# Gates and modulation vectors as sums along the row: one part of a two-layer diffusion block on one core

## The chip, the core and the metric

The kernel runs on one core of a Trainium2 chip. The core has five engines with an instruction queue each: TensorE (PE, matmuls, with its weight loads shown as PEld), VectorE (DVE), ScalarE (ACT), GpSimd (POOL) and SyncE (SP), and 16 DMA engines that move data between the chip's memory and the core's own. An engine runs its own queue in order; engines wait for each other through semaphores. The metric is the device time of one execution in microseconds. Before the change the median of three runs is 1769.55 us (1769.22 to 1769.56).

## What is computed

Two layers over 256 latent tokens with 2048 channels; the first also reads 256 context tokens. Each layer turns a conditioning vector into a shift, a scale and a gate per channel:

```python
def adaln(cond, w, b):
    m = jax.nn.silu(cond) @ w + b
    return jnp.split(m, 3, axis=-1)

def modulate(h, shift, scale):
    return h * (1 + scale) + shift

for i in range(DEPTH):                                   # DEPTH = 2
    shift, scale, gate = adaln(c, ada_w[i], ada_b[i])    # ada_w[i]: 2048 x 6144
    h = modulate(rms_norm(x, norm_g[i]), shift[:, None], scale[:, None])
    ...
    y = na_ssd_mixer(h, hc, ...) if i % 2 == 0 else short_conv_mixer(h, ...)
    x = x + gate[:, None] * y
```

The first layer's mixer has a wide input projection, 16 heads of neighbourhood attention, a bidirectional state-space scan, and an output projection. The second layer's has an input projection of 8192 columns, a short convolution, and an output projection. Everything is fp32.

The change concerns one thing: the products of the vector `silu(c)` with those parts of `ada_w` that aren't needed at the start. These are the first layer's gate (2048 columns) and the second layer's shift, scale and gate (6144 columns), 8192 columns in all, 64 MB of weights. The shift and scale of the first layer are made another way, at the start, and stay as they are.

## The kernel before

**Matmuls and weights.** Each fp32 weight is split into a high part in the format fp32r (ScalarE, L419) and the rest (VectorE, L426), and each product is made of three matmuls: high by high, low by high, high by low. L194 is the helper that records every matmul, L198 the one that records every transpose. Weights come in blocks of 128x1024 (512 KB) from SP's queue (L380 and L382) into buffers called `raw`: five of them, and four more at the start. A block waits there until one of three places `w` (six in the last part) is free, is split into it, used, and gives the place back.

**The order.** No scheduler runs on the chip. The program is laid out when it is built: generators for each piece of work say what they wait for, and a planner with its own cost for each instruction (class `Plan`, L38) decides which may put its next instructions on which engine. There are three lists, `urgent`, `side` and `back`. The vector-matrix products stand in `back`, the last to be asked (L283). When one generator changes, what the planner sees changes, and the instructions of all engines may be laid out anew.

**The products of the vector.** `later_loads` (L504) puts 128 loads of 128x1024 into a list: 16 groups `n` of 512 columns, eight loads `k` each, with two blocks of 128 rows beside each other, so that a partition holds two runs of 512 columns. `issue` (L364) sends them in among the ordinary weights, one or two under way at a time (`ngem`). `gemv_gen` (L799) consumes them, two groups at a time:

- VectorE clears `acc`, 128x1024 (L803). SP loads the bias, 512 numbers, into the first partition of each half (L808).
- For each load VectorE runs two instructions (L817) of 512 columns: weights times the channel's entry of `silu(c)` (the vector lies across the partitions in `csil`), plus `acc`.
- TensorE sums `acc` over the partitions with eight matmuls against ones (L825), VectorE copies the result to `rowb` (L827), and ScalarE's queue stores it as a row in `mrow` in the chip's memory (L830).
- After group 11 the shift and scale of the second layer are read back from there, transposed by TensorE into a column tile `M1` and copied (L835 to L840).

`n_back` says how far this has come. The gate of the first layer (from 3 on) is read in `res_gen` (L1587), `M1` (from 11.5 on) in `turn_gen` (L1625) and in `norm_gen` behind it, the gate of the second layer (from 15 on) in `fin_gen` (L1957). Gates are read from `mrow` as a row that is copied to all partitions.

**The rows that the prediction's steps touch.** L194, L198: matmuls and transposes. L419, L426: the split of a weight block. L603: the same kind of multiply-and-sum along the row that the change uses, in the norm of the input. L613, L628: the norm's scaling and the copy of its transposed tiles, at the start. L1910 to L1921: the second layer's gating. L1161: the first use of `rows` in the scan's time steps.

## Time and profile before

| | us |
|---|---|
| median of three runs | 1769.55 |
| profiled execution | 1768.15 |
| its span | 1766.2 |
| TensorE busy | 1742.5 |
| VectorE busy | 1260.7 |
| ScalarE busy | 773.2 |
| VectorE, the sums of L817 | 191.6 |
| VectorE, idle until a load of `ada_w` came | 64.2 |
| moved by DMA | 374.60 MB, mean 212 GB/s |

The profile is one execution. "Busy" is the time in which an engine has at least one instruction under way. Matmuls are pipelined and their ends are modelled, so the distance from one start to the next is the better measure of their cost. A group's line gives its line in the kernel, engine, operation, output and inputs with their shapes, the count, busy us and mean ns of one, and then the idle time of the engine just ahead of these instructions, with what ended it. The chain of waits follows the work that ended last backwards, at each step to what released it. A wait's line reads: who waited, for whom, us in all, times, longest. A line of the view by tile gives the shortest, median and longest duration in ns, and the first and the last start in us. Names lose their buffer numbers, so `tmp<-dram_csr` is any buffer `tmp` loaded from `dram_csr`.

### The profile page before, as it was taken

The page shows a single profiled execution, that of the slowest core. Times are in us where ns is not written, and L with a number is a line of the kernel's source. Part 1 is how long each engine was busy: PE and PEld are TensorE (multiplying, and loading weights), DVE is VectorE, ACT ScalarE, POOL GpSimd, SP SyncE. Part 2 cuts the span into 40 slices and gives each one's busy share as a digit, 9 for nine tenths or more (in the row PEclk, how much of TensorE's full clock was granted, in tenths as well). Part 3 has the DMA queues.
Part 4 walks back from the last instruction along what each step waited for, and adds up shares of the span by engine and source line. Part 5 has one row for each costly group of instructions (what it writes and reads, how often), then busy time and mean ns, then how long its engine had stood idle before and what let it go on. Part 6 is the DMA issues. An engine that isn't in the chain of part 4 may idle for free.

```text
span 1766.2 us, 25384 instructions
## 1 busy us (share of the span) xinstructions
PE 1742.5 (99%) x9577; PEld 1464.8 (83%) x9577; DVE 1260.7 (71%) x1986; ACT 773.2 (44%) x1330; POOL 32.1 (2%) x28
## 2 busy tenths in 40 slices
PE   6999999999999999999999999999999999999998
PEld 4777988888888889888888898888888888888887
DVE  5657778878686878675878787787668776555554
ACT  5423544455242445342445344565445444444442
POOL 0000100001000001000001000000000000000000
PEclk9999999999999999999999999999999999999999
DMA  9977644666746666646666566667867877666563
GB/s 369 347 283 253 209 148 134 200 207 203 233 141 199 205 199 194 220 134 195 209 189 190 159 189 198 194 207 273 294 212 239 264 260 250 189 187 189 190 210 120
DMA packets 218138, 374.60 MB, mean 212 GB/s; under 512 B 32304, under 2 KB 69008, under 8 KB 218016
## 3 DMA queue, kind: packets, MB, share of 16 engines
q1 hardware_dynamic: 210704, 366.38, 64.1%
q10 hardware_dynamic: 7312, 6.61, 1.1%
q8 instruction: 75, 1.23, 0.3%
q14 instruction: 47, 0.39, 0.1%
HBM read 367.52 MB, written 6.72 MB: 212 GB/s over the span
## 4 chain that ended last, share of the span: by engine, by line
PE 90%; DMA 5%; DVE 4%; issue 1%; SPq 1%; ACT 1%; POOL 0%; DVEq 0%; ACTq 0%
PE bank L194 86%; PE bank L198 3%; DMA raw<-in_ada_w 2%; DVE acc L817 1%; DVE w L426 1%; DMA tmp<-dram_csr 1%; DMA raw<-in_w_in 1%; DMA raw<-in_ada 0%; DVE tmp L1241 0%; DMA raw<-in_sc_in 0%; DMA half<-in_rows 0%; SPq L1045 0%; DMA acc<-in_ada_b 0%; ACT w L419 0%; DVE tmp L981 0%
## 5 line engine op out<-in xcount | busy, mean ns | idle before, releaser
L419 ACT CAST w<-raw 128x1024 fp32r<-128x1024 f32 (+1 forms) x343 | 358.2, 1046 | 536.4 <-PE bank L194 458.9
L426 DVE TENSOR_TENSOR w<-raw,w 128x1024 fp32r<-128x1024 f32 (+1 forms) x343 | 414.8, 1213 | 179.7 <-ACT w L419 178.4
L194 PE MATMUL bank<-hH,w 128*128 128x256 f32 (+1 forms) x2064 | 489.2, 324 | 2.5 <-DVE w L426 2.5
L194 PE MATMUL bank<-w,hH 128*128 128x512 f32 x1280 | 405.8, 395 | 2.6 <-ACT hH L757 2.6
L194 PEld LDWEIGHTS bank<-hH,w 128*128 128x128 f32 x2064 | 345.0, 188 | 36.0 <-DVE w L426 3.5
L194 PE MATMUL bank<-hL,w 128*128 128x256 f32 (+1 forms) x1040 | 334.3, 322 | 0.0
L194 PEld LDWEIGHTS bank<-w,hH 128*128 128x128 f32 x1280 | 236.6, 188 | 54.6 <-issue 4.6
L194 PE MATMUL bank<-w,hL 128*128 128x512 f32 x640 | 249.3, 390 | 0.1
L817 DVE SCALAR_TENSOR_TENSOR acc<-raw,csil,acc 128x512 f32<-128x512 f32 x256 | 191.6, 748 | 74.7 <-DMA raw<-in_ada_w 64.2
L194 PEld LDWEIGHTS bank<-hL,w 128*128 128x128 f32 x1040 | 196.4, 189 | 14.9
L194 PE MATMUL bank<-w,h 128*128 128x512 f32 x768 | 180.1, 391 | 0.0
L194 PEld LDWEIGHTS bank<-w,h 128*128 128x128 f32 x768 | 143.4, 188 | 29.8 <-issue 0.4
L194 PEld LDWEIGHTS bank<-w,hL 128*128 128x128 f32 x640 | 120.1, 188 | 25.4 <-DVE hL L763 0.6
L194 PE MATMUL bank<-w,mix 128*128 128x512 f32 x588 | 138.8, 392 | 0.0
L194 PEld LDWEIGHTS bank<-w,mix 128*128 128x128 f32 x588 | 109.4, 188 | 22.6 <-issue 0.2
L1241 DVE SCALAR_TENSOR_TENSOR tmp<-bank,cwh,tmp 128x508 f32<-128x508 f32 (+1 forms) x96 | 71.1, 744 | 1.8
L194 PE MATMUL bank<-KL,h 128*128 128x512 f32 x264 | 63.9, 389 | 0.0
L194 PEld LDWEIGHTS bank<-KL,h 128*128 128x128 f32 x264 | 49.5, 188 | 10.2
L426 DVE TENSOR_TENSOR wL<-raw,wH 128x1024 fp32r<-128x1024 f32 x31 | 37.9, 1222 | 27.6 <-ACT wH L419 27.5
L194 PE MATMUL bank<-QT,h 128*128 128x512 f32 x168 | 55.9, 391 | 0.0
L194 PE MATMUL bank<-wH,h 128*128 128x512 f32 x168 | 55.6, 390 | 0.0
L426 DVE TENSOR_TENSOR QL<-raw,QT 128x1024 fp32r<-128x1024 f32 x32 | 39.1, 1222 | 23.1 <-ACT QT L419 22.6
(288 smaller groups left out, 1976.8 us busy)
## 6 DMA issues: line engine op xcount, KB each, us to landing
raw<-in_w_in SPq DMA_DIRECT2D x196, 512.0 KB, 4.1
raw<-in_ada_w SPq DMA_DIRECT2D x128, 512.0 KB, 4.3
raw<-in_sc_in SPq DMA_DIRECT2D x128, 512.0 KB, 4.6
raw<-in_w_out SPq DMA_DIRECT2D x64, 512.0 KB, 4.2
raw<-in_ada SPq DMA_DIRECT2D x36, 512.0 KB, 5.4
raw<-in_sc_out SPq DMA_DIRECT2D x32, 512.0 KB, 3.7
PT<-in_ada SPq DMA_DIRECT2D x16, 512.0 KB, 8.6
tmp<-dram_csr SPq DMA_DIRECT2D x32, 256.0 KB, 5.8
```

Source lines behind the costliest of these rows:

```text
L194: E(T.matmul(o, l, r, start=start, stop=stop, skip_group_check=True))
L198: E(T.transpose(o, i, ident if k == 128 else ident[:k, :k]))
L419: E(S.copy(H, v))
L426: E(V.tensor_tensor(out=Lo, in0=v, in1=H.bitcast(F32), op=ALU.subtract))
L817: E(V.scalar_tensor_tensor(out=acc, in0=v[:, j], scalar=csil[:, 2 * k + j:2 * k + j + 1], in1=acc, op0=ALU.mult, op1=ALU.add))
L1241: E(V.scalar_tensor_tensor(out=do, in0=di, scalar=cwh[:, 32 * k + ch:32 * k + ch + 1], in1=do, op0=ALU.mult, op1=ALU.add))
```

## The change

The weights of these products are laid out anew on the host: block `m` of 128 output channels lies across the partitions, one channel to each, and the 2048 rows of the matrix lie along the row, in two halves of 1024. A load is still 128x1024, now in one piece. VectorE multiplies a block with `silu(c)`, which lies as a row in all partitions (`csb`), and sums along the row, in one instruction (L824 of the changed kernel). The result is one column of `gp` for each load. The two halves are added, then the bias, from a tile that is there anyway.

```diff
+    GEM = (range(0, 16), range(16, 48), range(48, 64))
...
-        for n in range(16):
-            lay = 0 if n < 4 else 1
-            c0 = 4096 + n * 512 if n < 4 else (n - 4) * 512
-            for k in range(8):
-                later.append(("g", ("gem", n, k), ada_w[lay], k * 256, 2, c0, 512))
+        for q, blocks in enumerate(GEM):
+            for h in range(2):
+                for m in blocks:
+                    later.append(("g", ("gem", m, h), adaT, 2 * m + h, 1, 0, 1024))
...
-    mrow = drt([4, D], "mrow")
+    mrow, crow = drt([2, D], "mrow"), drt([1, D], "crow")
     M1 = st([128, 2, KB], "M1")
-    accs = st([128, 2, 512], "acc")
+    csb = st([128, 1024], "csb")
+    gp = st([128, 2, 64], "gp")
+    rowt = st([128, 128], "rowt")
+    gcol = st([128, KB], "gcol")
...
+    def rows_out(col, dst):
+        yield W_("PE", col, nb=1)
+        ps = bank()
+        turn(ps[:16, :128], col)
+        yield W_("DVE", ps)
+        E(V.tensor_copy(rowt[:16, :], ps[:16, :128]))
+        give(free_b, ps)
+        yield W_("AQ", rowt)
+        E(DMA2.dma_start(dst.rearrange("(b c) -> b c", c=128), rowt[:16, :]))
...
     def gemv_gen():
-        for n2 in range(0, 16, 2):
-            yield W_("DVE", nb=0)
-            E(V.memset(accs, 0.0))
-            for n in (n2, n2 + 1):
...
-                    for j in range(2):
-                        if j:
-                            yield W_("DVE", acc)
-                        E(V.scalar_tensor_tensor(out=acc, in0=v[:, j], scalar=csil[:, 2 * k + j:2 * k + j + 1], in1=acc,
-                                                 op0=ALU.mult, op1=ALU.add))
+        yield from rows_out(csil[:, 0:KB], crow[0])
+        for q, blocks in enumerate(GEM):
+            for h in range(2):
+                yield W_("SP", crow, csb)
+                E(DMA.dma_start(csb, crow[0, h * 1024:(h + 1) * 1024].partition_broadcast(128)))
+                for m in blocks:
+                    yield when(lambda: ("gem", m, h) in RAW)
+                    yield W_("DVE", RAW["gem", m, h][0], csb)
+                    raw, _ = RAW.pop(("gem", m, h))
                     ngem[0] -= 1
+                    E(V.tensor_tensor_reduce(out=raw, in0=raw, in1=csb, scale=1.0, scalar=0.0, op0=ALU.mult, op1=ALU.add,
+                                             accum_out=gp[:, h, m:m + 1]))
                     give_raw(raw)
                     issue()
-            yield W_("PE", accs, nb=1)
-            ps = bank()
-            for m in range(2):
-                for g in range(4):
-                    mm(ps[32 * g:32 * g + 32, m * 128:(m + 1) * 128], ONES[:, :32], accs[:, m, g * 128:(g + 1) * 128], m == 0, True)
...
+            yield W_("DVE", gp)
+            p2 = lambda lo, n: (gp[:, 0, lo:lo + n], gp[:, 1, lo:lo + n])
+            if q == 1:
+                a, b = p2(16, 32)
+                o = M1.rearrange("p r b -> p (r b)")
+                E(V.tensor_tensor(out=o, in0=a, in1=b, op=ALU.add))
+                E(V.tensor_tensor(out=o, in0=o, in1=P_("ab1")[:, 0:32], op=ALU.add))
+            else:
+                a, b = p2(0 if q == 0 else 48, 16)
+                E(V.tensor_tensor(out=gcol, in0=a, in1=b, op=ALU.add))
+                E(V.tensor_tensor(out=gcol, in0=gcol, in1=P_("ab0" if q == 0 else "ab1")[:, 32:48], op=ALU.add))
+                yield from rows_out(gcol, mrow[q // 2])
+            n_back[0] = (3, 11.5, 15)[q]
```

The order of the parts stays: first layer's gate (`q` 0, 32 loads), second layer's shift and scale (`q` 1, 64 loads, straight into `M1`), second layer's gate (`q` 2, 32 loads). `csb` holds one half of the vector, so it is loaded six times, and each load has to wait for the last pass over the half before. The two gates, and `silu(c)` itself at the beginning, go through `rows_out`: a transpose on TensorE (16 columns of 128 to 16 rows), a copy on VectorE, a store from ScalarE's queue. The rest of the kernel is as before.

More of the change, by code (lines that the diff above doesn't have):

```diff
@@ L141, with kernel @@
 @with_exitstack
-def kernel(ctx: ExitStack, tc, x, cx, ada0, w0, ada_w, ada_b, w_in, w_out, sc_in, sc_out, rpb, small, const,
+def kernel(ctx: ExitStack, tc, x, cx, ada0, w0, adaT, w_in, w_out, sc_in, sc_out, rpb, small, const,
                        strict, rows, out):
@@ L378, in issue @@
             v = raw[:, :nb * n].rearrange("p (b c) -> p b c", b=nb)
-            if w is ada0 or w is w0:
+            if w is ada0 or w is w0 or w is adaT:
                 E(DMA.dma_start(raw, w[r0]))
@@ L791, in part_gen @@
         got.add(("part", j, key, t))
-    mrow = drt([4, D], "mrow")
+    mrow, crow = drt([2, D], "mrow"), drt([1, D], "crow")
     M1 = st([128, 2, KB], "M1")
-    accs = st([128, 2, 512], "acc")
+    csb = st([128, 1024], "csb")
+    gp = st([128, 2, 64], "gp")
+    rowt = st([128, 128], "rowt")
+    gcol = st([128, KB], "gcol")
     n_back = [0]
-    def gemv_gen():
-        for n2 in range(0, 16, 2):
-            yield W_("DVE", nb=0)
-            E(V.memset(accs, 0.0))
-            for n in (n2, n2 + 1):
-                lay = 0 if n < 4 else 1
-                c0 = 4096 + n * 512 if n < 4 else (n - 4) * 512
-                acc = accs[:, n - n2, :]
-                E(DMA.dma_start(acc[:1, :], ada_b[lay:lay + 1, c0:c0 + 512]))
-                for k in range(8):
-                    yield when(lambda: not (("gem", n, k) not in RAW))
-                    yield W_("DVE", RAW["gem", n, k][1], acc)
-                    raw, v = RAW.pop(("gem", n, k))
-                    ngem[0] -= 1
-                    for j in range(2):
-                        if j:
-                            yield W_("DVE", acc)
-                        E(V.scalar_tensor_tensor(out=acc, in0=v[:, j], scalar=csil[:, 2 * k + j:2 * k + j + 1], in1=acc,
-                                                 op0=ALU.mult, op1=ALU.add))
@@ L819, in gemv_gen @@
                     give_raw(raw)
                     issue()
-            yield W_("PE", accs, nb=1)
-            ps = bank()
-            for m in range(2):
-                for g in range(4):
-                    mm(ps[32 * g:32 * g + 32, m * 128:(m + 1) * 128], ONES[:, :32], accs[:, m, g * 128:(g + 1) * 128], m == 0, True)
-            yield W_("DVE", ps)
-            E(V.tensor_copy(rowb, ps[:, :256]))
-            give(free_b, ps)
-            yield W_("AQ", rowb)
-            E(DMA2.dma_start(mrow[n // 4, (n2 % 4) * 512:(n2 % 4) * 512 + 1024].rearrange("(m g c) -> g m c", m=2, g=4),
-                             two(rowb[0:128:32, :])))
@@ L832, in gemv_gen @@
-            n_back[0] = n
-            if n == 11:
-                yield W_("AQ", mrow[2:3, 1024:])
-                E(DMA2.dma_start(mrb[:32, :], mrow[1:3, :].rearrange("r (b c) -> (r b) c", c=128)))
-                yield W_("PE", mrb, nb=1)
-                pm = bank()
-                turn(pm[:, :32], mrb[:32, :])
-                yield W_("DVE", pm)
-                E(V.tensor_copy(M1.rearrange("p r b -> p (r b)"), pm[:, :32]))
-                give(free_b, pm)
-                n_back[0] = 11.5
@@ L844 @@
-    rowb = st([128, 256], "rowb")
-    mrb = rowb[:, :128]
+            yield W_("DVE", gp)
[10 more added lines that the diff above has]
+                yield from rows_out(gcol, mrow[q // 2])
@@ L1960, in fin_gen @@
         gb, o = tmp(), tmp()
-        yield W_("SP", mrow[3:4])
-        E(DMA.dma_start(gb, mrow[3, cols].partition_broadcast(128)))
+        yield W_("SP", mrow[1:2])
+        E(DMA.dma_start(gb, mrow[1, cols].partition_broadcast(128)))
         for t in range(2):
@@ L1995 @@
     force(lambda: not urgent, (urgent,))
-_INS = ['x', 'cx', 'ada0', 'w0', 'ada_w', 'ada_b', 'w_in', 'w_out', 'sc_in', 'sc_out', 'rpb', 'small', 'const', 'strict', 'rows']
+_INS = ['x', 'cx', 'ada0', 'w0', 'adaT', 'w_in', 'w_out', 'sc_in', 'sc_out', 'rpb', 'small', 'const', 'strict', 'rows']
 def kernel(**inputs):
@@ L2038 @@
                    for j in range(8) for c in (COL_K, COL_V, COL_Q)]).reshape(24, 128, 1024)
+    adaT = np.concatenate([f('ada_w')[0][:, 4096:], f('ada_w')[1]], axis=1).reshape(2, 1024, 64, 128).transpose(2, 0, 3, 1)
+    adaT = adaT.reshape(128, 128, 1024)
     arr = {
-        'x': f('x')[0], 'cx': f('ctx')[0], 'ada0': ada0, 'w0': w0, 'ada_w': f('ada_w'), 'ada_b': f('ada_b'), 'w_in': f('na_ssd_w_in')[0],
+        'x': f('x')[0], 'cx': f('ctx')[0], 'ada0': ada0, 'w0': w0, 'adaT': adaT, 'w_in': f('na_ssd_w_in')[0],
         'w_out': f('na_ssd_w_out')[0], 'sc_in': f('sc_w_in')[0], 'sc_out': f('sc_w_out')[0], 'rpb': f('na_rpb')[0],
```

## The prediction

> **What bounds the kernel now.** I read the page first: share of each engine, granted clock, the chain that ended last.

> ```profile
> span 1766.2 us, 25384 instructions
> PE 1742.5 (99%) x9577; PEld 1464.8 (83%) x9577; DVE 1260.7 (71%) x1986; ACT 773.2 (44%) x1330; POOL 32.1 (2%) x28
> PEclk9999999999999999999999999999999999999999
> PE 90%; DMA 5%; DVE 4%; issue 1%; SPq 1%; ACT 1%; POOL 0%; DVEq 0%; ACTq 0%
> ```

> TensorE is busy 99% of the span at full clock, and 90% of the chain is its own work. A microsecond of TensorE work is therefore a microsecond of the result, and work on VectorE costs time only where TensorE ends up waiting for it. Next I read the waits of TensorE that VectorE ended (first three rows; TensorE's other long wait, for the first weights, is at the start), and where they stand in the chain in order of time (start, length, what).

> ```profile
> PE bank L194 <- DVE w L426: 2.5, 2, 1.8
> PE bank L194 <- DVE tmp L1426: 1.1, 1, 1.1
> PE bank L198 <- DVE sgL L1916: 0.7, 1, 0.7
> ...
> 230.44 5.51 DMA half<-in_rows
> 236.40 1.21 DVE w L426
> 237.66 25.76 PE bank L194 x131
> ...
> 807.09 5.60 DMA raw<-in_ada_w
> ...
> 814.35 3.71 DMA raw<-in_ada_w
> ...
> 819.72 3.67 DMA raw<-in_ada_w
> ...
> 825.47 3.28 DMA acc<-in_ada_b
> ...
> 835.71 1.22 DVE w L426
> ...
> 842.56 7.82 PE bank L194 x64
> ...
> 1400.08 4.41 DMA raw<-in_ada_w
> ```

> All that VectorE holds TensorE up after the start is 2.5 + 1.1 + 0.7 = 4.3 us. The 1.8 us at 237 has nothing to do with the change: VectorE had sat behind the load of `rows`. The other 0.7 of the first row (842 us) and the 0.7 before 1410 us end stretches in which VectorE waited, again and again, for a load of `ada_w` that a sum over L817 needs, with the split of the weights (L426) queued behind it.

> **The change part by part.** The groups it touches (line, engine, operation, count | busy us, mean ns | idle before):

> ```profile
> L817 DVE SCALAR_TENSOR_TENSOR acc<-raw,csil,acc 128x512 f32<-128x512 f32 x256 | 191.6, 748 | 74.7 <-DMA raw<-in_ada_w 64.2 <-DMA acc<-in_ada_b 7.0
> L803 DVE MEMSET acc<- 128x1024 f32 x8 | 7.3, 912 | 1.3 <-issue 0.8 <-DVE half L1128 0.2 <-DMA raw<-in_w_in 0.2
> L827 DVE COPY rowb<-bank 128x256 f32<-128x256 f32 x8 | 3.4, 419 | 5.9 <-PE bank L194 5.9
> L194 PE MATMUL bank<-acc,const 128*32 128x128 f32 x128 | 5.2, 279 | 0.0
> L603 DVE CUSTOM_DVE_ANT_0 tmp<-x 128x512 f32<-128x512 f32 x8 | 5.3, 684 | 0.0
> L426 DVE TENSOR_TENSOR QL<-raw,QT 128x1024 fp32r<-128x1024 f32 x32 | 39.1, 1222 | 23.1 <-ACT QT L419 22.6
> ```

> *TensorE, removed.* 128 records are 8 groups of 16. Their mean of 279 ns is a modelled end; the price is read from start to start:

> ```profile
> 481.54 0.39 PE L194 MATMUL bank<-hL,w 128*128 128x512 f32 x1
> 481.77 0.39 PE L194 MATMUL bank<-hH,w 128*128 128x512 f32 x1
> 482.09 0.64 PE L194 MATMUL bank<-acc,const 128*32 128x128 f32 x16
> 482.66 0.50 PE L194 MATMUL bank<-hH,w 128*128 128x512 f32 x1
> 483.00 0.40 PE L194 MATMUL bank<-hL,w 128*128 128x512 f32 x1
> ...
> 1107.16 0.39 PE L194 MATMUL bank<-w,hL 128*128 128x512 f32 x1
> 1107.48 0.24 PE L198 MATMUL bank<-const,rowb 32*128 32x32 f32 x1
> 1107.65 0.73 PE L194 MATMUL bank<-w,hH 128*128 128x512 f32 x2
> 1108.22 0.39 PE L194 MATMUL bank<-w,hL 128*128 128x512 f32 x1
> ```

> Wide matmuls start 0.23 us apart. Without the group the one at 483.00 would start at 481.77 + 2 x 0.23 = 482.23, so a group costs 0.77 us, the change of shape on both sides included. Eight cost 6.2 us. The one transpose of `rowb`, by the same reading, costs 1108.22 - (1107.16 + 3 x 0.23) = 0.37 us. Removed: 6.6 us.

> *TensorE, added.* Three transposes of a 128x16 column tile (`csil`, and `gcol` twice). They are not in the trace; the nearest row is that 0.37 us. Bounds: 0.1 us each (a transpose that starts in step with its neighbours) to twice the row, 0.74. I take the row: 1.1 us in all, with 0.3 to 2.2 as ends. Net on TensorE: **-5.5 us** (-6.3 to -4.4).

> *VectorE.* Removed: 191.6 + 7.3 + 3.4 = 202.3 us. Added: 128 multiply-and-sum passes over 128x1024. The same operation over 128x512 takes 684 ns (L603), an elementwise pass over 128x1024 1222 ns (L426); I take 1.22 us. Each has a second instruction that reads the sum out:

> ```profile
> L603 DVE DVE_READ_ACCUMULATOR2_ANT ssq<- x8: 81/82/83, 6.7 to 35.9; 128x1 f32 x8
> ```

> So 1.30 us for each load of weights against 2 x 0.75 before: 166 us, and about 2 us for the few small additions and copies. Net -34 us, and nothing of it is on the path by itself. What it is worth are parts of the 4.3 us. The waits for `ada_b` (7.0 us of VectorE, among them the 3.28 us at 825) go; the memsets go; a cycle in the stretch before 842 gets 0.2 us shorter. In the changed program the last sum also stands behind 301 splits of weights instead of 357, so the stretch before 1410 us holds none. I count those two stalls as gone, -1.4 us. But the instructions of all engines are laid out anew by the planner, and a new layout has stalls of its own: VectorE-ended ones came to 4.3 us before. I add 0.7 us. Net **-0.7 us**; ends -4.3 (no such stall left) and +4.3 (twice as many).

> [...]

> *Loads and queues.* The 128 loads stay 512 KB each on SP, now with 4 KB in a row per partition. Gone are 16 small `ada_b` loads from SP and 8 row stores and a load from ScalarE's queue; new are 3 row stores there, and 6 broadcasts of 512 KB into `csb` on SP.

> ```profile
> raw<-in_ada_w SPq DMA_DIRECT2D x128, 512.0 KB, 4.3
> tmp<-dram_csr SPq DMA_DIRECT2D x32, 256.0 KB, 5.8
> ```

> A broadcast has to wait for the last pass over the old `csb`; SP holds every later weight load behind that, and the next pass on VectorE waits for the landing, with the splits queued behind it. The nearest price is between the two rows, 4.3 to 5.8 us. The first comes before any pass; five are exposed. In the stretch before 842 us the four waits shown above (5.60 to 3.28 us) held VectorE so within 22 us, and TensorE lost 0.7 us at its end, because it had split weights in hand. I cost five single waits at 0; ends 0 and five times that 0.7, +3.5 us. Without the cover each would cost its landing.

> *Start.* The store of `crow` is new in ScalarE's order, ahead of L628.

> ```profile
> 31.79 0.72 ACT L613 ACTIVATE x<-x,rx 128x512 f32<-128x512 f32 x1
> ...
> 32.41 0.38 PE L198 MATMUL bank<-const,x 128*128 128x128 f32 x2
> 32.82 0.27 ACT L628 COPY xm<-bank 128x128 f32<-128x128 f32 x1 [0.31 <-PE bank L198]
> ```
> ```profile
> L830 ACTq DMA_DIRECT2D dram_mrow<-rowb x8: 532/532/1092, 382.1 to 1498.8; - x8
> ...
> L1962 SPq DMA_DIRECT2D tmp<-dram_mrow x4: 423/468/1740, 1696.5 to 1744.3; - x4
> ```

> L628 waits for TensorE anyway, and the 0.53 us of an issue (L830) can run in the sequencer while L613 computes: 0; at most what 0.31 us of idle time leaves of it, 0.2. The memset that goes, at the place of the new copy, was the longer one.

> *Later.* The last row was stored at 1499 us and is first read at 1697; in the changed program the sums end earlier still. The first gate is finished at the same place in the order as before. Both stay covered, cost 0; uncovered, the price would be the whole lateness.

> Sum: -5.5 - 0.7 = **-6.2 us**. The profiled execution took 1768.15 us, its span and 1.95 around it; that gives 1761.95. The median of the runs lies 1.40 us above the profiled execution, so the prediction for the median is **1763.3 us**.

> **The rivals.** What a measurement of this kernel can tell from no change is about 0.2%, 3.5 us: below 1766.0 is faster, above 1773.1 slower.

> *The saved TensorE time turns into waiting.* The new layout has about twice the VectorE stalls and some broadcasts show: -5.5 + 4.3 + 1.5 is about 0, 1769. For it: the order was laid out anew everywhere. Against it: VectorE has 34 us less to do. [...] Chance 0.20.

> *More is won.* All VectorE stalls but the one behind `rows` go and the transposes cost little: -6.3 - 2.5 - 1, about 1760 or below. Chance 0.10.

> *Slower: the swap of `csb`.* At each of the five swaps SP holds the weight loads until VectorE has caught up, and VectorE holds the splits until 512 KB have landed; TensorE runs out. It decides from (5.5 + 3.5) / 5 = 1.8 us a swap. At 3 us a swap, about half the landing, it is +15 - 5.5: 1779. For it: VectorE waited 64 us for such loads before. Against it: four within 22 us cost 0.7. Chance 0.13.

> [...] Chance 0.05.

> **How the numbers follow.** The forecast keeps 0.52. Its own bounds are 1759 to 1768. Faster: 0.50 of the forecast, 0.10, and 0.05 of the first rival, 0.65. Same: 0.17. Slower: 0.13 + 0.05 = 0.18. The range for 8 in 10 is 1758.5 to 1771: the forecast, most of the gain case and the first rival; it leaves the slower ones out.

> **What would show it.** Right: the 16-matmul groups are gone and nothing stands in their place, so TensorE's busy time falls by about 5.5 us with no more idle time; the multiply-and-sum rows show about 1.22 us and 0.08; VectorE's busy time falls by some 34 us; no wait of TensorE traces back to `csb`. Wrong: new waits of TensorE for L427 (the old L426) behind a pass that waited for `csb` or a load; rows of 2 us; a later first wide matmul than at 34 us.

## The result, and the profile after

| | before | after |
|---|---|---|
| median, us | 1769.38 (six runs, 1767.05 to 1770.01) | 1786.65 (six runs, 1783.88 to 1789.53) |
| ratio, with its 95% interval | | 1.0101 (1.0086 to 1.0116) |
| profiled execution, us | 1768.15 | 1783.88 |

The changed kernel is 17 us slower; 6 us faster was predicted. The page of the changed kernel, with the lines that were read first before (span, busy time by engine, granted clock, shares of the chain):

```profile
span 1782.1 us, 25025 instructions
PE 1761.9 (99%) x9451; PEld 1467.8 (82%) x9451; DVE 1224.5 (69%) x1978; ACT 773.0 (43%) x1330; POOL 31.6 (2%) x28
PEclk9999999999999999999999999999999999999999
PE 98%; DVE 1%; DMA 1%; ACT 0%; issue 0%; SPq 0%; POOL 0%; DVEq 0%; ACTq 0%
```

TensorE has 126 matmul records fewer, and is busy for 19.4 us longer, at full clock (1.0 granted in both). It isn't waiting either: its own work is now 98% of the chain, against 90%. So the loss lies inside the work that the change doesn't touch. The new work itself looks as forecast. Its groups (count | busy us, mean ns | idle before), and then, from the waits of TensorE (us in all, times, longest), the only one that VectorE ends:

```profile
L824 DVE CUSTOM_DVE_ANT_0 raw<-raw,csb 128x1024 f32<-128x1024 f32 x128 | 155.4, 1219 | 21.3 <-DMA raw<-in_adaT 19.1 <-DMA csb<-dram_crow 1.9
L824 DVE DVE_READ_ACCUMULATOR2_ANT gp<- 128x1 f32 x128 | 10.5, 82 | 0.0
```

```profile
PE bank L195 <- DVE w L427: 0.9, 1, 0.9
```

A pass takes 1219 ns and its read-out 82, the swaps of `csb` cost VectorE 1.9 us in all, and what VectorE holds TensorE up fell from 4.3 us to 0.9.

What grew is shown by stretches of equal work in the chain of waits (start, length, number of matmuls). First the kernel before, then the changed one:

```profile
100.12 13.01 PE bank L194 x80
...
1631.51 43.54 PE bank L194 x192
1679.35 82.32 PE bank L194 x363
```

```profile
103.17 13.26 PE bank L195 x80
...
1644.83 43.74 PE bank L195 x192
1692.93 84.71 PE bank L195 x363
```

The last 363 matmuls of the second layer, which have nothing to do with the change, take 84.71 us in place of 82.32: 233.4 ns each in place of 226.8. The 192 before them keep 43.5 to 43.7. Over the whole trace, from one start to the next, the 5919 records of 512 columns sum to 1390.5 us against 1369.7, and the 2144 of 256 columns to 259.4 against 257.4. Together that is +22.8 us; less the 6 us that the change takes off, it is the 17 us. The wide matmuls that stayed at a median of 227 ns are most of those with a stationary operand `h1_*` and `mix19` to `mix31`; those on `hH`, on `y2` and on the other `mix` tiles went to 231 to 236.

What these operands have in common is their place in memory. The compiled programs give every tile's address. The change replaces `acc` and `rowb` (5120 bytes per partition) by `csb`, `gp`, `rowt` and `gcol` (4096 + 512 + 512 + 64), so every tile allocated behind them lies 64 bytes further: `hH0` to `hH15`, `hL0` and `hL1`, and what takes their places later (half of `mix`, `y2`, the first two of `h1_*`). The weights' places, `KL`, `QT`, and most of `hL` and `h1_*` lie ahead of them and stay.

### The profile page after: what moved, and what is told of

Same layout as the page of the kernel before. It is cut to its first block, busy times and chain, and to the rows that moved or that the text cites. A ratio compares the mean times of both kernels' runs of the same rounds, so it can differ in the third digit from the quotient of the medians.

```text
span 1782.1 us, 25025 instructions
## 1 busy us (share of the span) xinstructions
PE 1761.9 (99%) x9451; PEld 1467.8 (82%) x9451; DVE 1224.5 (69%) x1978; ACT 773.0 (43%) x1330; POOL 31.6 (2%) x28
## 3 DMA queue, kind: packets, MB, share of 16 engines
q8 instruction: 74, 1.21, 0.3%
## 4 chain that ended last, share of the span: by engine, by line
PE 98%; DVE 1%; DMA 1%; ACT 0%; issue 0%; SPq 0%; POOL 0%; DVEq 0%; ACTq 0%
PE bank L195 94%; PE bank L199 3%; DMA raw<-in_ada 0%; DMA raw<-in_sc_in 0%; DVE w L427 0%; SPq L583 0%; DVE KL L427 0%; DVE tmp L603 0%; DVE tmp L759 0%; DVE raw L824 0%; ACT KL L420 0%; ACT half L724 0%; ACT x L613 0%; DVE tmp L1963 0%; DVE tmp L1597 0%
## 5 line engine op out<-in xcount | busy, mean ns | idle before, releaser
L420 ACT CAST w<-raw 128x1024 fp32r<-128x1024 f32 x343 | 359.0, 1047 | 550.2 <-PE bank L195 452.5
L427 DVE TENSOR_TENSOR w<-raw,w 128x1024 fp32r<-128x1024 f32 x343 | 416.8, 1218 | 250.7 <-ACT w L420 249.4
L195 PE MATMUL bank<-hH,w 128*128 128x256 f32 (+1 forms) x2064 | 495.9, 327 | 0.9 <-DVE w L427 0.9
L195 PE MATMUL bank<-w,hH 128*128 128x512 f32 x1280 | 412.2, 400 | 2.6 <-ACT hH L757 2.5
L195 PE MATMUL bank<-hL,w 128*128 128x256 f32 (+1 forms) x1040 | 337.9, 325 | 0.0
L824 DVE CUSTOM_DVE_ANT_0 raw<-raw,csb 128x1024 f32<-128x1024 f32 x128 | 155.4, 1219 | 21.3 <-DMA raw<-in_adaT 19.1
L427 DVE TENSOR_TENSOR KL<-raw,KL 128x1024 fp32r<-128x1024 f32 x32 | 39.2, 1225 | 33.5 <-ACT KL L420 33.5
L427 DVE TENSOR_TENSOR wL<-raw,wH 128x1024 fp32r<-128x1024 f32 x31 | 38.0, 1225 | 34.3 <-ACT wH L420 34.3
L427 DVE TENSOR_TENSOR QL<-raw,QT 128x1024 fp32r<-128x1024 f32 x32 | 39.2, 1224 | 30.1 <-ACT QT L420 30.1
## 6 DMA issues: line engine op xcount, KB each, us to landing
raw<-in_w_in SPq DMA_DIRECT2D x196, 512.0 KB, 3.9
raw<-in_adaT SPq DMA_DIRECT2D x128, 512.0 KB, 4.7
raw<-in_sc_in SPq DMA_DIRECT2D x128, 512.0 KB, 3.7
raw<-in_w_out SPq DMA_DIRECT2D x64, 512.0 KB, 5.0
raw<-in_ada SPq DMA_DIRECT2D x34, 512.0 KB, 6.8
raw<-in_sc_out SPq DMA_DIRECT2D x32, 512.0 KB, 3.7
PT<-in_ada SPq DMA_DIRECT2D x16, 512.0 KB, 6.9
raw<-in_w SPq DMA_DIRECT2D x16, 512.0 KB, 6.3
```

Source lines behind the costliest of these rows:

```text
L195: E(T.matmul(o, l, r, start=start, stop=stop, skip_group_check=True))
L420: E(S.copy(H, v))
L427: E(V.tensor_tensor(out=Lo, in0=v, in1=H.bitcast(F32), op=ALU.subtract))
L824: E(V.tensor_tensor_reduce(out=raw, in0=raw, in1=csb, scale=1.0, scalar=0.0, op0=ALU.mult, op1=ALU.add, accum_out=gp[:, h, m:m + 1]))
```

## The experiments

Twelve kernels were run. The theories, as the expectations name them: **A**, an operand that starts off a multiple of 128 bytes is slow by itself; **B**, only the difference between the starts of a matmul's two operands counts; **C**, not the addresses but the new loads, passes or a lower clock; and later **D**, on where part of the gain went. Ratios are to runs of the kernel before on the same chip.

| run | what it is | median, us | ratio (95%) |
|---|---|---|---|
| e1 | changed, `gcol` padded to 128 bytes | 1781.01 | 1.0067 (1.0042 to 1.0091) |
| e2 | before, +64 bytes ahead of `hH0` | 1792.34 | 1.0132 (1.0106 to 1.0158) |
| e4 | before, +32 bytes ahead of `hH0` | 1790.46 | 1.0116 (1.0095 to 1.0137) |
| e5 | before, +64 bytes ahead of every tile | 1771.16 | 1.0001 (0.9987 to 1.0015) |
| e6 | changed, `gcol` padded to 256 bytes | 1764.42 | 0.9972 (0.9960 to 0.9983) |
| e7 | before, +256 bytes ahead of `hH0` | 1766.91 | 1.0000 (0.9983 to 1.0016) |
| e8 | before, a quarter of the `acc` matmuls | 1768.31 | 0.9998 (0.9987 to 1.0008) |
| e9 | e6, every pass of VectorE twice | 1775.59 | 1.0039 (1.0025 to 1.0054) |
| e10 | e6, passes held back 1.5 us | 1760.48 | 0.9956 (0.9942 to 0.9971) |
| e10 | e6, passes held back 3 us | 1758.55 | 0.9942 (0.9930 to 0.9955) |
| e11 | before, none of the `acc` matmuls | 1763.69 | 0.9972 (0.9961 to 0.9983) |
| e13 | changed, `gcol` ahead of every tile | 1762.94 | 0.9965 (0.9952 to 0.9979) |

### Moving tiles, changing nothing else

Each of these edits changes one allocation; the instructions and their order on every engine stay the same.

```diff
 e1 (changed kernel)
-    gcol = st([128, KB], "gcol")
+    gcol = st([128, 2 * KB], "gcol")[:, :KB]
 e2, e4 (kernel before; 8 columns more for e4)
-    rowb = st([128, 256], "rowb")
+    rowb = st([128, 272], "rowb")[:, :256]
 e5 (kernel before, ahead of the first tile)
+    pad = st([128, 16], "pad")
```

> The changed kernel with gcol padded from 64 to 128 bytes per partition: the same instructions in the same order, but every tile behind gcol (hH0 to hH15, hL0, hL1 and what later shares their places) starts at a multiple of 128 bytes again, as in the kernel before. Theory A (addresses: a matmul whose moving or stationary operand starts 64 bytes past a multiple of 128 runs slower) and theory B (addresses, but only the difference between the two operands' starts counts): the 512-column matmuls go back to 227 ns from start to start everywhere (233 in the changed kernel), about 21 + 2 us come back, and the time is 1763 us (1759 to 1767). Theory C (the new loads, the passes of VectorE or a lower clock slow TensorE): no change, 1785 us (1780 to 1790).

> The kernel before with 64 bytes added to rowb: nothing else differs, the tiles behind it (hH0 to hH15, hL0, hL1 and what shares their places) start 64 bytes past a multiple of 128, where the changed kernel has them. Theories A and B: the 512-column matmuls on these tiles take 231 to 236 ns from start to start in place of 227, 21 to 23 us in all, 1791 us (1785 to 1797). Theory C: no change, 1769 us (1766 to 1772).

> The kernel before with 32 bytes added to rowb, so that the same tiles start 32 bytes past a multiple of 128. Theories A and B leave the grain open: if only the place within 64 bytes counts, nothing or the same loss would be seen; if any start off a multiple of 128 costs, 1785 to 1797 us as with 64 bytes; if 32 bytes are harmless, 1769 us (1766 to 1772). Theory C: 1769 us.

> The kernel before with 64 bytes added ahead of the first tile, so that every tile moves by 64 bytes: all operands of the 512-column matmuls start 64 bytes past a multiple of 128, and the differences between them stay as they were. Theory A: all of them slow, also those between 1400 and 1600 us that the change left at 227 ns: 5900 by 4 to 6 ns, 1793 to 1805 us. Theory B: 227 ns everywhere, 1769 us (1766 to 1772). Theory C: 1769 us.

With 64 bytes of padding and nothing else, the kernel before loses 1.32%, more than the whole change does. That ends theory C. In e5 every operand of the wide matmuls is 64 bytes off a multiple of 128, and nothing is lost (ratio 1.0001): that ends theory A. But e1, expected back at 1763 us, came to 1781. Its tiles are 128 bytes from where they were before, and its wide matmuls take 232 ns. So B holds, with a grain coarser than 128 bytes, which e1's expectation had wrong. The last 363 matmuls in the chain of e2, e4, e1 and e5, in this order:

```profile
1700.01 84.71 PE bank L194 x363
```

```profile
1701.47 84.71 PE bank L194 x363
```

```profile
1688.63 84.70 PE bank L195 x363
```

```profile
1682.19 82.32 PE bank L195 x363
```

64, 32 and 128 bytes cost the same (84.7 us against 82.32 in the kernel before); a common shift costs nothing (82.32). Next came 256 bytes, in both kernels:

```diff
 e6 (changed kernel)
-    gcol = st([128, KB], "gcol")
+    gcol = st([128, 4 * KB], "gcol")[:, :KB]
 e7 (kernel before)
-    rowb = st([128, 256], "rowb")
+    rowb = st([128, 320], "rowb")[:, :256]
```

> The changed kernel with gcol padded to 256 bytes per partition, so that hH0 to hH15, hL0 and hL1 start a multiple of 256 bytes from the tiles of the weights, as they do in the kernel before. Theory B, now with the grain of 256 bytes that the first four runs gave: every 512-column matmul at 227 ns again, and the time is what the change is worth by itself: by the prediction's terms 1763 us (1760 to 1766). If a grain larger than 256 bytes counts, or a difference of exactly zero modulo 512 or 1024: 1775 to 1787 us, as with 64 and 128 bytes. Theory C (loads, passes of VectorE or the clock): 1785 us.

> The kernel before with 256 bytes added to rowb, the control to the runs with 64 and 32 bytes. Theory B with a grain of 256 bytes: no change, 1769 us (1767 to 1772), 227 ns. If any move of these tiles costs: 1785 to 1793 us.

Both are as theory B with a grain of 256 bytes has them: e7 doesn't differ from the kernel before, and e6 is 1764.42 us, 22 us below the changed kernel for 192 bytes of padding. The last run does it without padding:

```diff
 e13 (changed kernel)
+    gcol = st([128, KB], "gcol")
     free_t = [st([128, 512], f"tmp{k}") for k in range(NTMP)]
...
-    gcol = st([128, KB], "gcol")
```

> The changed kernel with gcol (64 bytes) laid ahead of the first tile in place of behind rowt: not a byte more, hH0 to hH15 at the same addresses as in the changed kernel, but the tiles of the weights and of hL2 on now also 64 bytes further, so that the differences are multiples of 256 bytes again. Theory B (the difference of the two operands' starts, modulo 256 bytes): 227 ns everywhere, 1764 us (1760 to 1767). Theory A (each operand's own start): every 512-column matmul at 231 to 236 ns, 1785 to 1800 us. Theory C: 1786 us.

Here `hH0` to `hH15` lie at the very addresses of the changed kernel, and the other operands were moved to fit them. The page, and the last 363 matmuls:

```profile
span 1760.1 us, 25025 instructions
PE 1736.7 (99%) x9451; PEld 1462.8 (83%) x9451; DVE 1224.6 (70%) x1978; ACT 773.0 (44%) x1330; POOL 31.6 (2%) x28
```

```profile
1673.32 82.32 PE bank L196 x363
```

The same 9451 records as in the changed kernel take 1736.7 us in place of 1761.9. To sum up, the distance between starts of 512-column matmuls, by the difference modulo 256 bytes between the start of the stationary operand that comes next and that of the moving operand. It is taken where the matmul, the one ahead of it and the two behind it are of this form, with each distance cut at 260 ns so that stalls don't count, and without groups of under 100:

```
run      difference   count   median ns   mean ns
before        0        5421      227       227.3
e7            0        5421      227       227.4
e5            0        5421      227       227.3
e6            0        5437      227       227.4
e13           0        5437      227       227.3
e4            0        2545      227       228.4
after         0        2556      227       229.2
e2            0        2545      227       229.4
e1            0        2556      227       228.3
e4           32        2139      232       233.1
after        64        2143      233       232.8
e2           64        2139      233       232.5
e1          128        2901      232       232.7
after       192         738      233       232.5
e2          192         737      233       232.4
e4          224         737      232       232.3
```

Where all operands differ by multiples of 256 bytes it is 227 ns, and at every other difference tried 232 or 233. But the four rows at 0 of kernels with moved tiles aren't uniform. In the changed kernel 1601 of the 2556 have only multiples of 256 around them and take 227.1 ns; the other 955 stand beside a matmul whose operands are off, and take 232.8 themselves (230.5 to 233.1 in the other three). So a matmul pays for its neighbours' operands too: in the changed kernel those with `hL2` to `hL15`, which haven't moved, but stand between matmuls on `hH`, are slow as well.

Whether it is the stationary operand in use or the one being loaded for the next matmul stays open. About a fifth of these matmuls have one of the two off and the other not, and in the changed kernel both kinds are slow: 232.9 ns with only the next one off (527 of them), 233.0 with only the one in use (539).

### What the change is worth, and where the rest of it went

With the addresses mended the change gains 0.28% (e6) and 0.35% (e13), 5 and 6 us, against the 6.2 predicted. To see which terms carry that, the removed matmuls were priced in the kernel before. e8 leaves out three quarters of them and e11 all, so neither computes the gates and modulation rightly. In both, the planner also lays out the other engines' instructions anew, so their times aren't the price of these matmuls alone.

```diff
 e8 (kernel before)
-                for g in range(4):
+                for g in range(1):
...
-            E(V.tensor_copy(rowb, ps[:, :256]))
+            E(V.tensor_copy(rowb[:32], ps[:32, :256]))
...
+    E(V.memset(rowb, 0.0))
 e11 (kernel before)
-            yield W_("PE", accs, nb=1)
-            ps = bank()
-            for m in range(2):
-                for g in range(4):
-                    mm(...)
-            yield W_("DVE", ps)
-            E(V.tensor_copy(rowb, ps[:, :256]))
-            give(free_b, ps)
+            yield W_("DVE", accs)
+            E(V.tensor_copy(rowb, accs[:, 0, :256]))
```

> The kernel before with a quarter of the matmuls that sum acc over partitions (32 of 128 records; the other three rows of each block of gates and modulation are left out, so the output is not the reference's); all addresses as before. It prices the TensorE term by itself: by the prediction 8 groups lose 12 of 16 records, 12/16 of 0.77 us each, 4.6 us in all: 1764.8 us (1762 to 1767). If the gaps beside such a group were filled by other work anyway: 1769 us.

> The kernel before without any of the 128 matmuls that sum acc over partitions (the sums are left out: the row is copied from acc itself, so the output is not the reference's); all addresses as before. A quarter of them cost as much as all (the trace of that run has 4.4 us for 32 records against 4.6 us for 128), since the four 32-column tiles of a group run side by side; without any the whole of it should go: 4.6 us of starts plus about 1 us beside them, 1763 to 1765 us. If the time saved on TensorE turns into waiting for VectorE's sums and loads: 1767 to 1769 us, with more waits of TensorE for L426.

The expectation of e8 was wrong. Its trace around a group (start, length, what; compare the rows at 481.77 to 482.66 us in the prediction):

```profile
481.46 0.39 PE L194 MATMUL bank<-hH,w 128*128 128x512 f32 x1
481.78 0.62 PE L194 MATMUL bank<-acc,const 128*32 128x128 f32 x4
482.34 0.50 PE L194 MATMUL bank<-hH,w 128*128 128x512 f32 x1
482.68 0.40 PE L194 MATMUL bank<-hL,w 128*128 128x512 f32 x1
```

Four records hold TensorE for 482.34 - 481.78 = 0.56 us, sixteen held it for 482.66 - 482.09 = 0.57. The price is one of the group, as the prediction had taken it from starts, and not one of the record, as e8 assumed: the four 32-column tiles run side by side (in the kernel before, the starts of such four lie within 0.02 us, and the next four follow after 0.11 to 0.13). Without the groups (e11) 0.28% is gained, 5 us, within its expectation.

The other question was whether VectorE's work is really covered.

```diff
 e9 (e6, behind each pass)
+                    E(V.tensor_tensor_reduce(out=raw, in0=raw, in1=csb, scale=1.0, scalar=0.0, op0=ALU.mult, op1=ALU.add,
+                                             accum_out=gcolt[:, 3 * KB:3 * KB + 1]))
```

> The changed kernel with gcol padded to 256 bytes, and behind each of the 128 multiply-and-sum passes a second one on raw with itself, whose sum goes to a spare column (it leaves the output's meaning behind, since only its time is wanted): 128 x 1.3 = 166 us more of VectorE, 1224 to 1390 us of busy time. If VectorE's work is hidden behind TensorE, as the prediction has it, it is within 5 us of the run without the second passes (1763 to 1768 us). If VectorE is close to being the bound in the stretches with these passes: 1775 us or more, with waits of TensorE for the weights' split on L427.

Nobody reads the second sums; the second pass multiplies by `csb` once more, and not by itself as the expectation has it. VectorE's busy time rose to 1373.8 us, and the time by 11 us over e6, most of it idle time of TensorE (span less busy time: 33.9 us against 24.5). That is the second branch of the expectation, at its lower end: VectorE's work isn't free in all places. TensorE's waits in e9 name the places:

```profile
PE bank L195 <- DVE half L1453: 4.0, 1, 4.0
PE bank L195 <- DVE w L427: 3.7, 3, 2.2
...
PE bank L199 <- POOL r L1466: 2.1, 1, 2.1
```

They are few and long, where the scan's chain runs through VectorE. Such a place is in e6 as well. The stretch from 1100 to 1130 us in four kernels (time, busy us of PE, PEld, DVE, ACT and POOL with counts, granted clock, DMA share, GB/s): the kernel before, the changed one, e6, e13.

```profile
1100.00:1130.00 30.00, 30.00 (x133) 24.56 (x132) 20.80 (x44) 18.32 (x41) 0.00 (x0) 1.00 0.60 185
```

```profile
1100.00:1130.00 30.00, 30.00 (x133) 24.23 (x132) 22.19 (x46) 15.40 (x35) 0.00 (x0) 1.00 0.83 265
```

```profile
1100.00:1130.00 30.00, 26.14 (x108) 20.91 (x107) 19.98 (x40) 15.13 (x34) 0.00 (x0) 0.95 0.73 240
```

```profile
1100.00:1130.00 30.00, 27.43 (x120) 22.20 (x119) 21.91 (x44) 16.42 (x37) 0.00 (x0) 1.00 0.76 253
```

TensorE loses 3.9 us there in e6 and 2.6 in e13. The granted clock dips in e6 (0.95), but not in e13 (1.00), so the dip isn't what makes the stall. The chain of e6 up to that stall, and VectorE's waits for the loads of the passes in e6:

```profile
1094.32 1.22 DVE raw L824
1095.57 6.54 DMA raw<-in_adaT
...
1105.44 10.17 DMA tmp<-dram_csr
...
1123.69 0.35 DVE raw L824
1124.04 0.70 issue
1124.74 0.08 DVE gp L824
1124.83 1.15 DVE w L427
```

```profile
DVE raw L824 <- DMA raw<-in_adaT: 28.1, 27, 2.5
```

A pass stands on VectorE ahead of its load, and the split that TensorE needs stands behind the pass. The changed kernel has the same instructions in the same order; there TensorE was slower, loads and splits kept ahead of it (19.1 us of such waits), and this stall wasn't there. Theory D says that these waits take part of the gain. The test lets the planner give a pass out only when it reckons the load to be some time old; only `gemv_gen` stands in the queue that this term concerns.

```diff
 e10 (e6; 1500 for the first of the two)
-            rdy += 4000 if eng == "PE" else 0
+            rdy += 4000 if eng == "PE" else 3000 if eng == "DVE" else 0
```

> The changed kernel with gcol padded to 256 bytes, and the planner holding back each multiply-and-sum pass until it reckons the load of adaT to be 1.5 us old (a term in the due time of the queue in which only gemv_gen stands). Theory D (part of the saved time has turned into waiting: the passes stand on VectorE ahead of their loads and delay what is queued behind them, as around 1095 to 1126 us of the run with 256 bytes, where TensorE lost 3.9 us): VectorE's waits for adaT fall from 28 us to under 15, that stall goes, and the time is 1760 to 1763 us against 1764.4 us. Rival (the stall comes from the load of dram_csr that took 10.2 us, whatever the passes do): 1764 us, the stall stays.

> The same with 3 us. Theory D: waits for adaT under 8 us, 1759 to 1762 us. Rival: 1764 us. If holding the passes back delays the loads of the weights behind them (the places for raw come free later): 1766 us or more.

With 3 us, VectorE's waits for these loads, the stretch from 1100 to 1130 us, and the page:

```profile
DVE raw L824 <- DMA raw<-in_adaT: 4.8, 10, 1.1
```

```profile
1100.00:1130.00 30.00, 30.00 (x155) 25.06 (x154) 23.43 (x48) 18.92 (x42) 0.00 (x0) 1.00 0.71 234
```

```profile
span 1756.9 us, 25008 instructions
PE 1736.4 (99%) x9451; PEld 1462.6 (83%) x9451; DVE 1222.8 (70%) x1978; ACT 773.2 (44%) x1330; POOL 31.7 (2%) x28
```

The stall is gone, and 1758.55 us is the fastest of all kernels run: 0.58% below the kernel before, 28 us below the changed one, and 0.45 us below what was expected. With 1.5 us the stall is gone too, the time lies between, and its interval overlaps e6's; the waits were 19.8 us, where under 15 was expected. That the held passes did it isn't shown. The planner lays out the other engines anew as well here, and the loads of `dram_csr` between 1080 and 1135 us landed in at most 7.1 us (7.5 with 1.5 us), against 10.2 in e6 and 9.5 in e13. In e13 the chain into the stall goes through that load of 9.5 us and not through one of `adaT`. So a stall that stays whatever the passes do is out, but how much of it is the passes and how much the `dram_csr` load stays open.

## Why the prediction was wrong

**The step that failed** is a silent one: "Wide matmuls start 0.23 us apart" was read off the kernel before and used for the changed one too. TensorE's term held the instructions that go and come, -5.5 us, and took for granted that the 8063 records of 512 and 256 columns that stay keep their pace. They didn't: +22.8 us, since the 64 bytes of `gcol` moved one operand against the other in over half of them, and the neighbours of these slowed with them. None of the rivals had it. "TensorE's busy time falls by about 5.5 us" came out as +19.4, and that pointed to the place. There was a sign in the code: the kernel before puts the weights of some stages 16 columns, 64 bytes, further into their places (`shifted`), which does nothing for what is computed.

**TensorE, removed and added** (-5.5): right. With the addresses mended, busy time fell by 5.8 us (e13: 1736.7 against 1742.5). Without the removed groups the kernel before gains about 5 us (e11; 6.2 in the sum), and e8 shows why the start-to-start reading was the right one.

**VectorE's busy time** (-34 us; passes of 1.22 and 0.08 us): right, -36.2 us, 1219 and 82 ns. The 0.05 among the slower outcomes was the author's estimate for passes of 2 us; the changed kernel shows none, and its longest pass took 1229 ns.

**VectorE on the path** (-0.7): near in size by luck, since the stalls left are others than those counted. TensorE's waits that VectorE ends after the start are 2.8 us in e6 and e13, against 4.3 before and 3.6 in the sum; the stall near 1125 us has a wait for ScalarE's split as well, 2.4 us in e6 and 1.1 in e13. e10 shows that more was to be had, as in the rival "More is won", but by an edit that the change doesn't make.

**The swaps of `csb`** (0): right, one wait of 1.9 us on VectorE in the changed kernel, between 700 and 1000 us, where TensorE waits for nothing of VectorE's.

**Start** (0): right within what kernels of one layout differ by. The wide matmul at 34.14 us starts at 34.75 in the changed kernel and 34.65 in e13, but also at 34.58 in e7 and 35.29 in e2, which have the instructions of the kernel before.

**The sum**, 1763.3 us, would have been right for a kernel whose tiles kept their differences: e6 has 1764.42, e13 1762.94.

## What to carry to other kernels

When a change adds, drops or resizes any buffer, list which tiles behind it move, and compare the starts of the two operands of the matmuls that carry the time, modulo 256 bytes, before and after (here 227 ns at a multiple of 256, 232 to 233 at the other differences tried); a small buffer can cost more than the change gains (the 64 bytes of `gcol` cost 22 us, by e6 against the changed kernel; the change is worth 5 to 6), and belongs ahead of all operands (e13) or behind them. When busy time of an engine at full clock grows with fewer instructions, compare equal stretches of work it shares with the kernel before, start to start, before looking at the new work. A price per instruction taken from a group must be tried on the group: here sixteen `acc` matmuls held TensorE for 0.57 us and four for 0.56 (e8), and 5 us were gained only without any of them (e11).

## What the runs showed of the hardware

**For 256 columns it isn't the same.** Their mean distance (cut at 1.3 times the median) is 115.9 ns at a difference of 64 bytes (1825 records before) and 118.3 at 0 (1271 in the changed kernel), 119.6 at 32 (1263 in e4) and 118.4 at 192 (1271 in e1). The kernel shifts some weights by 64 bytes there, and the change undid that for most of these matmuls, which goes with the +2.0 us. But the difference alone doesn't sort them: the 562 that keep 64 bytes in the changed kernel take 118.1 ns, and 164 at 224 bytes take 116.7 in the kernel before. No run leaves the shift out, so what it is worth, and which difference is best here, stays open.
